# Two-layer hybrid decoder on one core: where in SBUF the split weights and the feed-forward products' operands lie

## The chip, the cores and the metric

The kernel runs on one core of one Trainium2 chip. The metric is the device time of one execution in microseconds.

## The reference

Two layers, x of 256 tokens by 1024 channels, float32. In each layer a token mixer and a feed-forward follow one another, each with a residual and a layer norm:

```python
proj = x @ w_in        # RNN input | RNN gate | q latent | kv latent | rotary key | gate A | gate B
y_rnn = gelu(g_rnn) * rg_lru(causal_dwconv(x_rnn), ...)
y_mla = mla_attention(q_lat, kv_lat, k_rope_raw, ...)      # 16 heads, causal
x = layer_norm(ALPHA * x + (sigmoid(gate_a) * y_rnn + sigmoid(gate_b) * y_mla) @ w_out)
h_gate, h_val = split(causal_dwconv(x @ w_up))             # 2 x 3072 channels
x = layer_norm(ALPHA * x + (gelu(h_gate) * h_val) @ w_down)
```

## The kernel before, in words

Every large product is made of three float32r matmuls. An operand is split into a high part (ScalarE, line 185 for weights, line 199 for activations) and the rest, the low part (VectorE, lines 186 and 200); `mm3` (lines 193 to 196) adds high by high, high by low and low by high.

Weights come in blocks of 2048 columns by a DMA on SP's queue into one of four `raw` buffers (line 156). `load_split` cuts a block into two halves of 1024 and gives each half a buffer that holds its high and its low part. Weights used as stationary operand go to the pool `wpool`, tag "w": six buffers, any half in any of them. The down-projection's and some other weights go to the general slots of 4,096 bytes (`slot`). A raw buffer is free for the next DMA when both halves are split, a weight buffer when TensorE has read it for the last time.

`proj_pair` computes 256 channels by 256 tokens: for each of two groups of 128 channels (m) it goes over the eight chunks kc of the 1024 input channels, with three matmuls each, so 48 matmuls of 128x256. Chunks 0 to 3 lie in the first half's buffer, 4 to 7 in the second's. The moving operand is x. There are 16 such pairs in a layer's mixer (branches g and x, gates A and B, four each) and 22 in its feed-forward; the feed-forward's first two of 24 pairs are done by tokens (`up_tok`, tile upt, weights moving).

In the feed-forward `up(j)` makes the pair, the convolution and the gated product, and splits that into `hh` and `hl` (tag "k1", 13 buffers of 1,024 bytes). From the sixth pair on, each pair is followed by `out_chunk`: 12 matmuls of 128x512 into `dacc`, with a piece of `hh` or `hl` as stationary operand and the down weights in slots as moving one. There are 48 chunks, 576 such matmuls; 36 pairs come right behind a product. The tag "k1" also holds the splits of the RNN branch's convolution (`xch`, `xcl`), the transposed layer norm (`lnx`) and the merged branches (`mg`).

TensorE's order is the program's: the mixer's steps are written out by hand in `ORDER` (x is a pair of the RNN branch, e its gates, h a pair of gate B, b, q, k, p a group of heads, v its values, s, f, y attention, o the output projection). Loads are issued on SP in program order. ScalarE's and VectorE's order is made by a planner when the program is built.

The addresses follow from the pools, which lie one behind the other. The six weight buffers begin at 58,560 bytes of each partition and are 8,320 bytes apart; 58,560 is 192 modulo 256 and 8,320 is 128 modulo 256, so they lie at 192 and 64 in turn. All slots, so x, the down weights and the mixers' results, and all "k1" buffers lie at 0 modulo 256. Which buffer a half gets is settled when the program is built. Of the 36 pairs behind a product, 12 have both halves at the same place modulo 256, 18 the first at 192 and the second at 64, and 6 the first at 64 and the second at 192. An offset inside a half is a multiple of 512 bytes in all pairs.

Of the kernel before, what the change touches and what calls it, by code (L numbers as in the profile page):

```python
# [11 lines left out]
F32 = mybir.dt.float32  # L12
F32R = mybir.dt.float32r
# [4 lines left out]
P = 128  # L18
D = 1024
S = 256  # L20
# [29 lines left out]
HELD = 4  # L50
WARM = 8
LINE = 256
STEP = 32
KORD = (0, 1, 4, 5, 2, 3, 6, 7)
NPAIR = DFF // P
ALPHA = (2 * DEPTH) ** 0.25
# [69 lines left out]
def trunk(ctx, tc, x_tok, x_chan, pos, wts, par, lnrow, consts, out):  # L126
# [8 lines left out]
    wpool = ctx.enter_context(tc.tile_pool(name="wpool", bufs=1))  # L135
    big = ctx.enter_context(tc.tile_pool(name="big", bufs=1))
    sm = ctx.enter_context(tc.tile_pool(name="sm", bufs=2))
    pp = ctx.enter_context(tc.tile_pool(name="pp", bufs=4, space=bass.MemoryType.PSUM))

    def slot(name, dt=F32):  # L140
# [20 lines left out]
    def behind(ins, first):  # L161
        if first is not None:
            tc.add_manual_dep(ins.ins, first.ins.name, no_sync, reason="issue order")

    last_split = [None]
    ready = [(None, None)]
    later = [False]

    def load_split(l, key, cuts, in_slots=False, after=(None, None),
                   step=1024, parts=None, between=None):  # L170
        raw = load_raw(l, key, parts, between)
        if later[0]:
            after = ready[0]
        n = WOFF[key][1]
        res = []
        for a, b in cuts:
            if in_slots:
                hi, lo = slot("wsh", F32R), slot("wsl", F32R)
            else:
                both = wpool.tile([P, 2048 + STEP], F32R, tag="w", name="w", bufs=6)  # L180
                hi, lo = both[:, :1024], both[:, 1024:2048]
            for c in range(a, b, step):
                d = min(c + step, b)
                h, w = hi[:, c - a:d - a], raw[:, c:d]
                behind(A.activation(h, w, AF.Copy), after[0])  # L185
                lo_ins = V.tensor_tensor(out=lo[:, c - a:d - a], in0=w, in1=h.bitcast(F32),  # L186
                                         op=ALU.subtract)
                behind(lo_ins, after[1])
                last_split[0] = lo_ins
            res.append((hi, lo))  # L190
        return res
# [186 lines left out]
    class LayerNorm:  # L378
# [48 lines left out]
        def turn(self, t):  # L427
            l, z = self.l, self.res[t]
            ts = slice(t * P, (t + 1) * P)
            pts = [bank("lnT") for _ in range(2)]  # L430
            for q in range(2):
                for c in range(4):
                    T.transpose(pts[q][:, c * P:(c + 1) * P],
                                z[:, (4 * q + c) * P:(4 * q + c + 1) * P], ident)
            ea = None
            for cc in range(2):
                for q in range(2):
                    hi, lo = (v.rearrange("p (c s) -> p c s", c=4) for v in self.xs[q])
                    xt = sm.tile([P, 2, P], F32, tag="k1", name="lnx", bufs=13, align_bytes=LINE)
                    hv, lv = hi[:, 2 * cc:2 * cc + 2, ts], lo[:, 2 * cc:2 * cc + 2, ts]  # L440
                    for e in range(2):
                        c = 2 * cc + e
                        gc = pcol(l, self.gn, 4 * q + c)
                        bc = pcol(l, self.bn, 4 * q + c)
                        src = pts[q][:, c * P:(c + 1) * P]
                        if q == 0:
                            V.tensor_scalar(out=xt[:, e], in0=src, scalar1=gc, scalar2=bc,
                                            op0=ALU.mult, op1=ALU.add)
                        else:
                            behind(A.activation(xt[:, e], src, AF.Identity, scale=gc, bias=bc),  # L450
                                   ea)
                    ea = A.activation(hv, xt, AF.Copy)
                    ev = V.tensor_tensor(out=lv, in0=xt, in1=hv.bitcast(F32), op=ALU.subtract)
            self.ends = (ea, ev)
# [56 lines left out]
    for l in range(DEPTH):  # L511
# [6 lines left out]
        def proj_pair(key, r=None):  # L518
            if r is None:
                if key not in held:  # L520
                    fetch(key)
                r = held.pop(key)
            ps = bank("proj")
            for m in range(2):
                for kc in range(KC):
                    hi, lo = r[kc // 4]
                    o = (kc % 4) * 256 + m * P
                    rh, rl = xsl(xs, kc)
                    mm3(ps[:, m * S:(m + 1) * S], hi[:, o:o + P], lo[:, o:o + P],
                        rh, rl, kc == 0, kc == KC - 1)  # L530
            return ps

        gl = [slot("gl") for _ in range(2)]
# [61 lines left out]
        def conv_branch(i):  # L595
            ps = proj_pair(("x", i))
            for m in range(2):
                c = 2 * i + m
                dst = xc[c // 4][:, (c % 4) * S:(c % 4) * S + S]
                src = ps[:, m * S:(m + 1) * S]  # L600
                A.activation(dst, src, AF.Identity, scale=pcol(l, "cw", 24 + c),
                             bias=pcol(l, "cb", c))
                for k in range(1, 4):
                    conv_end.append(V.scalar_tensor_tensor(
                        out=dst[:, k:], in0=src[:, :S - k], scalar=pcol(l, "cw", 8 * (3 - k) + c),
                        in1=dst[:, k:], op0=ALU.mult, op1=ALU.add,
                    ))
                xh = sm.tile([P, S], F32R, tag="k1", name="xch", bufs=13, align_bytes=LINE)
                xl = sm.tile([P, S], F32R, tag="k1", name="xcl", bufs=13, align_bytes=LINE)
                A.activation(xh, dst, AF.Copy)  # L610
                V.tensor_tensor(out=xl, in0=dst, in1=xh.bitcast(F32), op=ALU.subtract)
                xsp[c] = (xh, xl)
# [181 lines left out]
        def values(c):  # L794
            g, pr = divmod(c, 2)
            pts = pst.pop(c)
            vs = vts[g // 2][1]
            yps = bank("yps")
            for t in range(NT):
                for hh in range(2):  # L800
                    hv = t * 512 + (4 * (g % 2) + 2 * pr + hh) * 64
                    T.matmul(yps[hh * 64:hh * 64 + 64, t * P:S], lhsT=vs[:, hv:hv + 64],  # L802
                             rhs=pts[hh][:, 2 * t * P:(2 + t) * P],
                             start=t == 0, stop=t == 1)
            if mer[c // 4] is None:
                mer[c // 4] = (slot("mhi", F32R), slot("mlo", F32R))
            cs = slice((c % 4) * S, (c % 4) * S + S)
            mg = sm.tile([P, S], F32, tag="k1", name="mg", bufs=13, align_bytes=LINE)
            V.tensor_tensor(out=mg, in0=yps[:, :S], in1=sB[c // 4][:, cs], op=ALU.mult)
            V.tensor_tensor(out=mg, in0=mg, in1=r_t[c // 4][:, cs], op=ALU.add)  # L810
            split2(mer[c // 4][0][:, cs], mer[c // 4][1][:, cs], mg)
# [76 lines left out]
        def up(j):  # L888
            if j < NB:
                ps = turn(j)  # L890
            else:
                r = uw.pop(j, None)
                if r is None:
                    r = load_split(l, ("up", j), ((0, 1024), (1024, 2048)), after=convs[max(0, len(convs) - 4)])
                ps = proj_pair(("up", j), r)
            u = []
            for m in range(2):
                ch = m * NPAIR + j
                src = ps[:, m * S:(m + 1) * S]
                dst = sm.tile([P, S], F32, tag="k15", name=f"u{m}", bufs=7,  # L900
                              align_bytes=LINE)
                ea = A.activation(dst, src, AF.Identity, scale=pcol(l, "fw", 96 + ch),  # L902
                                  bias=pcol(l, "fb", ch))
                for k in range(1, 3):
                    ev = V.scalar_tensor_tensor(  # L905
                        out=dst[:, k:], in0=src[:, :S - k],
                        scalar=pcol(l, "fw", 48 * (2 - k) + ch),
                        in1=dst[:, k:], op0=ALU.mult, op1=ALU.add,
                    )
                u.append(dst)  # L910
            convs.append((ea, ev))
            A.activation(u[0], u[0], AF.Gelu_apprx_tanh)
            V.tensor_tensor(out=u[1], in0=u[1], in1=u[0], op=ALU.mult)  # L913
            mh = sm.tile([P, S], F32R, tag="k1", name="hh", bufs=13, align_bytes=LINE)
            ml = sm.tile([P, S], F32R, tag="k1", name="hl", bufs=13, align_bytes=LINE)
            split2(mh, ml, u[1])
            hq[j] = (mh, ml)

# [145 lines left out]
```

## Time and profile before

| | |
|---|---|
| three runs | 785.43, 785.65, 787.75 us; median 785.65 us |
| the profiled execution | 786.62 us, of which the span from the first to the last instruction is 784.76 us |
| TensorE, matmuls | busy 770.5 us of the span |
| VectorE, ScalarE | busy 646.0 us, 510.2 us |
| DMA | 144.76 MB, 184 GB/s on average |
| granted TensorE clock | 0.995 of full speed over the span |

How to read it: a matmul's time in the trace reaches from its start to the end of its results and overlaps with the next one; what a matmul costs in a row of matmuls is the distance from its start to the next one's start. The page's busy time counts overlapping matmuls once. Times in the timeline are in microseconds from the span's start.

### The profile page before, as it was taken

What the parts mean: (1) busy time and instruction counts of PE and PEld (TensorE: products, weight loads), DVE (VectorE), ACT (ScalarE), POOL (GpSimd) and SP (SyncE); (2) the same over time, 40 slices, a digit from 0 to 9 for tenths busy, and PEclk for the clock granted to TensorE, in tenths of its full rate; (3) what the DMA queues carried; (4) which work ended last, traced back from release to release, by engine and by line L of the source; (5) the groups of instructions that cost most, each with busy time, mean ns of one, the idle gap of its engine ahead of it and who ended that gap; (6) DMA issues with size and microseconds to landing.
All of it is one profiled execution on the core that took longest, in us unless ns stands there. A gap on an engine that the chain in (4) does not pass through costs nothing.

```text
span 784.8 us, 14452 instructions
## 1 busy us (share of the span) xinstructions
PE 770.5 (98%) x5712; PEld 723.9 (92%) x5712; DVE 646.0 (82%) x1260; ACT 510.2 (65%) x910; POOL 10.2 (1%) x27
## 2 busy tenths in 40 slices
PE   9999899999999999999999999999999999999996
PEld 9999899878999999999899999998799999999994
DVE  6998789997699977668777897999877998677665
ACT  6856887783677565556374579688657775565540
POOL 0000000000000000000000000000000000000000
PEclk9999999999999999999999999999999999999999
DMA  9855436525457555535715554463515675746311
GB/s 320 331 210 215 151 112 240 207 63 210 162 199 262 203 199 210 195 126 196 268 52 218 169 208 134 172 231 123 193 76 186 261 251 182 247 162 200 123 54 54
DMA packets 26467, 144.76 MB, mean 184 GB/s; under 512 B 3360, under 2 KB 7072, under 8 KB 11808
## 3 DMA queue, kind: packets, MB, share of 16 engines
q1 hardware_dynamic: 26400, 143.84, 51.7%
q8 instruction: 45, 0.74, 0.4%
q14 instruction: 22, 0.18, 0.1%
HBM read 140.68 MB, written 1.05 MB: 181 GB/s over the span
## 4 chain that ended last, share of the span: by engine, by line
PE 89%; DVE 4%; ACT 4%; issue 2%; DMA 1%; SPq 0%; DVEq 0%
PE proj L196 16%; PE proj L194 15%; PE proj L195 15%; PE dacc L194 6%; PE dacc L195 6%; PE dacc L196 6%; PE oacc L194 2%; PE oacc L196 2%; PE oacc L195 2%; PE sps L759 2%; DVE w L186 2%; PE yps L802 2%; PE ptp L787 1%; PE latp L195 1%; PE latp L196 1%
## 5 line engine op out<-in xcount | busy, mean ns | idle before, releaser
L196 PE MATMUL proj<-xhi,w 128*128 128x256 f32 x1216 | 338.0, 278 | 3.0 <-DVE w L186 3.0
L194 PE MATMUL proj<-xhi,w 128*128 128x256 f32 x1216 | 338.1, 278 | 0.0
L195 PE MATMUL proj<-xlo,w 128*128 128x256 f32 x1216 | 337.7, 278 | 0.0
L186 DVE TENSOR_TENSOR w<-raw,w 128x1024 fp32r<-128x1024 f32 (+5 forms) x226 | 241.8, 1087 | 52.4 <-ACT w L185 51.9
L185 ACT ACTIVATE w<-raw 128x1024 fp32r<-128x1024 f32 (+5 forms) x226 | 208.8, 952 | 86.6 <-PE proj L196 73.4
L196 PEld LDWEIGHTS proj<-xhi,w 128*128 128x128 f32 x1216 | 228.8, 188 | 3.4 <-DVE w L186 3.4
L195 PEld LDWEIGHTS proj<-xlo,w 128*128 128x128 f32 x1216 | 229.2, 189 | 1.3
L194 PEld LDWEIGHTS proj<-xhi,w 128*128 128x128 f32 x1216 | 228.9, 188 | 1.4
L905 DVE SCALAR_TENSOR_TENSOR u<-proj,par,u 128x255 f32<-128x255 f32 (+1 forms) x176 | 83.4, 478 | 25.4 <-ACT u L902 23.3
L902 ACT ACTIVATE u<-proj,par 128x256 f32<-128x256 f32 x88 | 49.7, 564 | 72.7 <-DVE u L905 47.8
L194 PE MATMUL dacc<-wsh,hh 128*128 128x512 f32 x192 | 75.2, 392 | 0.0
L195 PE MATMUL dacc<-wsl,hh 128*128 128x512 f32 x192 | 75.1, 391 | 0.0
L196 PE MATMUL dacc<-wsh,hl 128*128 128x512 f32 x192 | 74.7, 389 | 0.0
L186 DVE TENSOR_TENSOR wsl<-raw,wsh 128x1024 fp32r<-128x1024 f32 (+2 forms) x66 | 70.4, 1077 | 0.0
L185 ACT ACTIVATE wsh<-raw 128x1024 fp32r<-128x1024 f32 (+2 forms) x66 | 59.5, 938 | 0.0
L196 PEld LDWEIGHTS dacc<-wsh,hl 128*128 128x128 f32 x192 | 36.1, 188 | 7.8
L194 PEld LDWEIGHTS dacc<-wsh,hh 128*128 128x128 f32 x192 | 36.0, 188 | 6.4
L195 PEld LDWEIGHTS dacc<-wsl,hh 128*128 128x128 f32 x192 | 36.1, 188 | 6.0
L199 ACT ACTIVATE hh<-u 128x256 fp32r<-128x256 f32 x48 | 19.8, 411 | 24.7 <-DVE u L913 24.6
L194 PE MATMUL oacc<-w,mhi 128*128 128x512 f32 x64 | 26.7, 417 | 0.0
L196 PE MATMUL oacc<-w,mlo 128*128 128x512 f32 x64 | 25.3, 395 | 0.0
L195 PE MATMUL oacc<-w,mhi 128*128 128x512 f32 x64 | 25.2, 393 | 0.0
(213 smaller groups left out, 1130.2 us busy)
## 6 DMA issues: line engine op xcount, KB each, us to landing
raw<-in_wts SPq DMA_DIRECT2D x114, 1024.0 KB, 4.9
raw<-in_wts SPq DMA_DIRECT2D x8, 832.0 KB, 4.9
gb<-in_lnrow SPq DMA_DIRECT2D x8, 512.0 KB, 7.7
raw<-in_wts SPq DMA_DIRECT2D x4, 672.0 KB, 4.0
raw<-in_wts SPq DMA_DIRECT2D x7, 336.0 KB, 6.1
raw<-in_wts SPq DMA_DIRECT2D x4, 512.0 KB, 4.8
xres<-in_x_tok SPq DMA_DIRECT2D x2, 512.0 KB, 6.0
k<-krot SPq DMA_DIRECT2D x8, 128.0 KB, 2.4
```

Of the source, the lines that this page charges most:

```text
L185: behind(A.activation(h, w, AF.Copy), after[0])
L186: lo_ins = V.tensor_tensor(out=lo[:, c - a:d - a], in0=w, in1=h.bitcast(F32), op=ALU.subtract)
L194: T.matmul(o, lhsT=lh, rhs=rh, start=start, stop=False)
L195: T.matmul(o, lhsT=lh, rhs=rl, start=False, stop=False)
L196: T.matmul(o, lhsT=ll, rhs=rh, start=False, stop=stop)
L199: A.activation(hi, src, AF.Copy)
L759: T.matmul(sps[:, P:P + S], lhsT=q96[:, h4, P:], rhs=k96[:, h4], start=True, stop=True)
L787: T.transpose(ptp[:, b * P:(b + 1) * P], sns[hh][:, b * P:(b + 1) * P], ident)
L802: T.matmul(yps[hh * 64:hh * 64 + 64, t * P:S], lhsT=vs[:, hv:hv + 64], rhs=pts[hh][:, 2 * t * P:(2 + t) * P], start=t == 0, stop=t == 1)
L902: ea = A.activation(dst, src, AF.Identity, scale=pcol(l, "fw", 96 + ch), bias=pcol(l, "fb", ch))
L905: ev = V.scalar_tensor_tensor(out=dst[:, k:], in0=src[:, :S - k], scalar=pcol(l, "fw", 48 * (2 - k) + ch), in1=dst[:, k:], op0=ALU.mult, o ...
```

## The change

The weight pool has two tags of three buffers, w0 for the first half of a block and w1 for the second, of 8,192 bytes each, with a tile of 128 bytes between them that is never used. By the pools' arithmetic w0 lies at 192 and w1 at 64 modulo 256. `proj_pair` goes over the chunks in the order 0, 4, 5, 1, 2, 3, 6, 7. The tiles of tag "k1" move to a pool of their own behind the others, after an unused tile of 160 bytes, and lie at 128 modulo 256. Blocks with one cut (the values' weights) use w0 alone.

```diff
-STEP = 32
+GAP = 32
+PORD = (0, 4, 5, 1, 2, 3, 6, 7)
...
+    kpool = ctx.enter_context(tc.tile_pool(name="kpool", bufs=1))
+    kpool.tile([P, 40], F32, name="kgap")
...
-        for a, b in cuts:
+        for i, (a, b) in enumerate(cuts):
             if in_slots:
                 hi, lo = slot("wsh", F32R), slot("wsl", F32R)
             else:
-                both = wpool.tile([P, 2048 + STEP], F32R, tag="w", name="w", bufs=6)
+                if i and not gap:
+                    gap.append(wpool.tile([P, GAP], F32, name="gap"))
+                both = wpool.tile([P, 2048], F32R, tag=f"w{i % 2}", name=f"w{i % 2}", bufs=3)
                 hi, lo = both[:, :1024], both[:, 1024:2048]
...
-                    xt = sm.tile([P, 2, P], F32, tag="k1", name="lnx", bufs=13, align_bytes=LINE)
+                    xt = kpool.tile([P, 2, P], F32, tag="k1", name="lnx", bufs=13)
...
             for m in range(2):
-                for kc in range(KC):
+                for kc in PORD:
                     hi, lo = r[kc // 4]
                     o = (kc % 4) * 256 + m * P
                     rh, rl = xsl(xs, kc)
                     mm3(ps[:, m * S:(m + 1) * S], hi[:, o:o + P], lo[:, o:o + P],
-                        rh, rl, kc == 0, kc == KC - 1)
+                        rh, rl, kc == PORD[0], kc == PORD[-1])
...
-            mh = sm.tile([P, S], F32R, tag="k1", name="hh", bufs=13, align_bytes=LINE)
-            ml = sm.tile([P, S], F32R, tag="k1", name="hl", bufs=13, align_bytes=LINE)
+            mh = kpool.tile([P, S], F32R, tag="k1", name="hh", bufs=13)
+            ml = kpool.tile([P, S], F32R, tag="k1", name="hl", bufs=13)
```

The tiles `xch`, `xcl` and `mg` change in the same way as `lnx`.

## Rows read from the trace of the kernel before

**Rows 1.** The page's first part: busy us, share of the span, instructions of each engine.

```profile
PE 770.5 (98%) x5712; PEld 723.9 (92%) x5712; DVE 646.0 (82%) x1260; ACT 510.2 (65%) x910; POOL 10.2 (1%) x27
```

**Rows 2.** TensorE's waits: engine, line, for whom; us in total, times, longest.

```profile
PE proj L196 <- DVE w L186: 3.0, 2, 1.5
PE gates L195 <- DVE xcl L611: 1.9, 2, 1.4
```

**Rows 3.** Busy time by stage, both feed-forwards: us, each engine, clock, DMA share, GB/s.

```profile
227.00:377.00 150.00, 150.00 (x1081) 141.26 (x1080) 121.86 (x190) 91.45 (x138) 0.00 (x0) 1.00 0.59 209
...
612.00:760.00 148.00, 148.00 (x1076) 139.18 (x1075) 117.19 (x183) 86.69 (x131) 0.00 (x0) 1.00 0.55 192
```

**Rows 4.** TensorE's timeline (start, us): a pair's first matmul, the next pair's first.

```profile
216.08 0.28 PE L194 MATMUL proj<-xhi,w 128*128 128x256 f32 x1
...
221.52 0.28 PE L194 MATMUL proj<-xhi,w 128*128 128x256 f32 x1
```

**Rows 5.** TensorE's timeline: first matmul of a pair at 64 and 64, the product behind.

```profile
237.96 0.28 PE L194 MATMUL proj<-xhi,w 128*128 128x256 f32 x1
...
243.62 0.40 PE L194 MATMUL dacc<-wsh,hh 128*128 128x512 f32 x1
```

**Rows 6.** TensorE's timeline: pair at 192 and 64, its matmuls 1, 13, 16, the product behind.

```profile
229.71 0.28 PE L194 MATMUL proj<-xhi,w 128*128 128x256 f32 x1
...
231.12 0.28 PE L194 MATMUL proj<-xhi,w 128*128 128x256 f32 x1
...
231.48 0.28 PE L194 MATMUL proj<-xhi,w 128*128 128x256 f32 x1
...
235.22 0.40 PE L194 MATMUL dacc<-wsh,hh 128*128 128x512 f32 x1
```

**Rows 7.** TensorE's timeline: first matmul of a pair at 64 and 192, the product behind.

```profile
622.84 0.28 PE L194 MATMUL proj<-xhi,w 128*128 128x256 f32 x1
...
628.38 0.40 PE L194 MATMUL dacc<-wsh,hh 128*128 128x512 f32 x1
```

**Rows 8.** TensorE's timeline: first matmuls of layer 1's first and second pair.

```profile
410.08 0.28 PE L194 MATMUL proj<-xhi,w 128*128 128x256 f32 x1
...
415.73 0.28 PE L194 MATMUL proj<-xhi,w 128*128 128x256 f32 x1
```

**Rows 9.** TensorE's timeline: third gate-B pair of layers 0, 0 and 1, matmuls 3, 13, 3.

```profile
116.95 0.38 PE L196 MATMUL proj<-xhi,w 128*128 128x256 f32 x1 [1.51 <-DVE w L186]
...
118.24 0.28 PE L194 MATMUL proj<-xhi,w 128*128 128x256 f32 x1
...
502.05 0.38 PE L196 MATMUL proj<-xhi,w 128*128 128x256 f32 x1 [1.51 <-DVE w L186]
```

**Rows 10.** VectorE's timeline: splits around the third gate-B pair and layer 0's last pair.

```profile
113.56 5.34 DVE L186 TENSOR_TENSOR w<-raw,w 128x896 fp32r<-128x896 f32 x5
...
370.72 1.21 DVE L186 TENSOR_TENSOR w<-raw,w 128x1024 fp32r<-128x1024 f32 x1
```

**Rows 11.** ScalarE's timeline: a branch-x pair's first half, the second head group's queries.

```profile
64.87 1.06 ACT L185 ACTIVATE w<-raw 128x1024 fp32r<-128x1024 f32 x1 [2.61 <-issue]
...
114.73 0.84 ACT L185 ACTIVATE w<-raw 128x768 fp32r<-128x768 f32 x1
```

**Rows 12.** TensorE's timeline: matmuls 1 and 6 of the first feed-forward product.

```profile
226.96 0.40 PE L194 MATMUL dacc<-wsh,hh 128*128 128x512 f32 x1
...
228.12 0.39 PE L196 MATMUL dacc<-wsh,hl 128*128 128x512 f32 x1
```

**Rows 13.** TensorE's timeline: two matmuls of an output projection, four steps apart.

```profile
177.67 0.39 PE L195 MATMUL oacc<-w,mhi 128*128 128x512 f32 x1
...
178.60 0.39 PE L196 MATMUL oacc<-w,mlo 128*128 128x512 f32 x1
```

**Rows 14.** TensorE's timeline: two matmuls of the up-projection by tokens, four steps apart.

```profile
196.96 0.28 PE L194 MATMUL upt<-wsh,xhi 128*128 128x256 f32 x1
...
197.44 0.28 PE L195 MATMUL upt<-wsl,xhi 128*128 128x256 f32 x1
```

More of the change, by code (lines that the diff above doesn't have):

```diff
@@ L163, in behind @@
             tc.add_manual_dep(ins.ins, first.ins.name, no_sync, reason="issue order")
+    gap = []
     last_split = [None]
@@ L607, in conv_branch @@
                     ))
-                xh = sm.tile([P, S], F32R, tag="k1", name="xch", bufs=13, align_bytes=LINE)
-                xl = sm.tile([P, S], F32R, tag="k1", name="xcl", bufs=13, align_bytes=LINE)
+                xh = kpool.tile([P, S], F32R, tag="k1", name="xch", bufs=13)
+                xl = kpool.tile([P, S], F32R, tag="k1", name="xcl", bufs=13)
                 A.activation(xh, dst, AF.Copy)
@@ L807, in values @@
             cs = slice((c % 4) * S, (c % 4) * S + S)
-            mg = sm.tile([P, S], F32, tag="k1", name="mg", bufs=13, align_bytes=LINE)
+            mg = kpool.tile([P, S], F32, tag="k1", name="mg", bufs=13)
             V.tensor_tensor(out=mg, in0=yps[:, :S], in1=sB[c // 4][:, cs], op=ALU.mult)
```

## Prediction

> **What bounds the kernel now.** I read the page's first part, TensorE's waits and the busy time by stage, then the order of single matmuls in time. TensorE is busy 770.5 us, 98% of the span [rows 1]; what it waits for others inside the work is 3.0 us for weight splits and 1.9 us for the gates' input, all in the mixers [rows 2], the rest of its idle time lies at both ends of the program. In both feed-forward stretches it is busy without a break (150.00 of 150.00 us and 148.00 of 148.00), while VectorE has 28 and 31 us to spare [rows 3]. So the time is the sum of the steps from one matmul's start to the next, and the question is what sets a step.
>
> The same product, 128x256 of proj, has two steps. A whole pair (48 matmuls) took 221.52 - 216.08 = 5.44 us, 113.3 ns a step [rows 4]; another took 243.62 - 237.96 = 5.66 us, 117.9 ns [rows 5]. Shapes, operands, the granted clock (full, 2.4 GHz [rows 3]) and even the place of the weights are the same, both halves at 64 modulo 256, and neither pair holds a wait. What differs is what ran before: the quick pair follows a quick pair, the slow one a feed-forward product. So the step depends on a state that is carried from matmul to matmul, and the buffers show where it changes. A third pair, first half at 192 and second at 64, begins slow (12 matmuls in 231.12 - 229.71 = 1.41 us), takes 0.36 us for three more after the move to 64, and has 113.3 ns a step from there to its end (33 in 235.22 - 231.48 = 3.74 us): 5.51 us in all [rows 6]. With 64 first and 192 second it took 628.38 - 622.84 = 5.54 us [rows 7]: there the step falls only at the return to 64 in the middle. The starts of all 76 pairs follow this, but for one that is released only at its third quarter. Once quick, a pair stays quick through every change of buffer; a slow one is released by going from 192 to 64, not by going from 64 to 192, and one without a change stays slow to the end. Every pair that follows a feed-forward product begins slow.
>
> Of the 36 such pairs, 12 keep to one class (5.65 to 5.66 us, 0.21 over 5.44), 6 go from 64 to 192 (0.10 over), 18 from 192 to 64 (0.07 over), each kind within 0.01 us of its row [rows 4 to 7]: 2.5 + 0.6 + 1.3 = 4.4 us. In layer 1's mixer the first three pairs are slow throughout (the first from 410.08 to 415.73, 5.65 us [rows 8]), 0.6 us, and the pair after the long wait of layer 0 loses 0.2 us.
>
> **The change, part by part.**
>
> *Weight buffers and order.* By the sizes, w0 starts at 58,560 (192 modulo 256, three of 8,192 bytes keep that), the gap adds 128 bytes, so w1 is at 64. Every pair goes from 192 to 64. In the new order the first such move comes after 3 matmuls and not 12, and there are four in a pair. Taking rows 6 as the rule, a pair that begins slow loses 3 x 4.5 ns before the move and the three steps of 0.12 us after it (about 15 ns): 0.028 us. The 36 pairs go from 4.4 to 1.0 us: -3.4. The three of layer 1's mixer: -0.55; the one of layer 0: -0.15. Together **-4.1 us**.
>
> *The second half is wanted sooner.* Before, its first use comes 12 matmuls (1.36 us) into a pair, now 3 (0.34 us). Where weights are ready long ahead this costs nothing; the cover is the distance of several us from the split to its use in the proj stretches. It costs where a pair waits for its own split. In both mixers that is the third pair of branch gate B: its third matmul starts at 116.95 and 502.05, after VectorE has written the first half's low part [rows 9]. VectorE then has two of five splits in a row left (they end at 113.56 + 5.34 = 118.90 [rows 10]); the second half's low part is the fourth, done about 118.05 at some 1.15 us each, and as far behind in layer 1. Before, that half's first matmul started at 118.24 [rows 9]. Now its low part is wanted at 117.4, so TensorE, which issues in order, stands about 0.65 us longer in each layer: **+1.3 us**, 0 if VectorE's order puts that split sooner, +2.0 if the first split slips too. The last pair of layer 0's feed-forward has its second half's low part ready 0.4 us after the pair begins (at 370.72 + 1.21 = 371.93, and that pair then wants it 0.56 us after its begin at 371.51 [rows 10]); with its first half released later (next part) I add **+0.3**, between 0 and 0.7.
>
> *Three buffers for each half in place of six for all.* The first half's last read is now chunk 3 in sixth place, two chunks (0.68 us) later. ScalarE's split into that buffer waits for it: at 64.87 it had stood idle 2.61 us, until the pair then running had read its first half [rows 11]. There the chain runs on through VectorE to the gates, for which TensorE waits [rows 2]. So up to 0.65 us in layer 0; I take **+0.4**, from 0 (VectorE has rope work to put in) to 1.5 (two or three splits in a row late by 0.65 before that wait). In attention a value block and a held output block also take first-half buffers. The split of 114.73 [rows 11] then waits for the third gate-B pair's first half, some 7 us; behind it on ScalarE stand the queries' and keys' copies, unless the planner, which orders ScalarE and VectorE anew, puts them ahead. By the same count the weights are still ready 3 us or more before use, and SP's loads wait for raw buffers that the second half's split frees, as before. Nothing for those; +2 if the new order is worse.
>
> *Feed-forward products' stationary tiles from 0 to 128 modulo 256*, moving weights at 0. No row has a 512-wide matmul with the two 128 apart. Now a block of 12 takes 1.16 us for its first five steps, 232 ns each, and then settles at 227 (seven in 229.71 - 228.12 [rows 6, 12]). Over 38 blocks the first five lose up to 0.026 us each, some 0.9 us. Low end: that goes, -0.9. Upper end: the nearest row is the output projection, whose moving weights are 64 or 192 apart from the stationary operand and which doesn't settle: 0.93 us for four steps, 232 [rows 13], so +5 ns on the 7 to 12 steps of a block that are now at 227, some +2.2 us over 576 steps. Far end: a product with both at 0 takes 120 ns a step and not 113.3 (four in 0.48 us [rows 14]); in that proportion the 512-wide would take 240, +6.7. I take **0**, as settled runs there are the rule, and keep -0.9 and +6.7.
> The Trainium skill, "TensorE: Matmul & The Clock Gate", section "Back-to-back issue gap", gives N/2.4 + 2.5 ns, which is 215.8 for 512. By it 576 such steps have 6 us in hand; no 512-wide float32r step of this trace is under 225.
>
> *The other tiles in the new pool* (conv splits, normalised x, merged) are read by TensorE only in 96 gate matmuls: nothing, between -0.1 and +0.4.
>
> **Sum.** -4.1 + 1.3 + 0.3 + 0.4 + 0 = -2.1 us. The profiled execution took 786.62 (span 784.76 and 1.86 around it), so 784.5; the median of the three runs, 785.65, lies 0.97 below it, so **783.5 us**.
>
> **Rivals.**
> 1. *The products lose at 128.* Each of 576 steps on a path that TensorE alone sets becomes longer. For: the output projection doesn't settle with other offsets. Against: the products settle within five steps at 0. Price on the forecast: at 232 ns +2.2, 785.7; at 236, +4.5, 788.0; at 240, 790.2. It ends slower than before by over 0.3% from a mean of 236 ns. 0.17, half of it above 788.
> 2. *More is won.* The pairs start quick, as the stationary tile read just before now lies elsewhere (-1.0), the products lose their slow first steps (-0.9), and the two waits for the second half don't come (-1.3): 780.3. For: what a pair starts with follows what ran before it. Against: VectorE's order follows the program. 0.18.
> 3. *The addresses do nothing*, and the slow steps come from something else in those stretches. Against: the step falls at a move from 192 to 64 in 24 of the pairs behind a product and never at another place [rows 6, 7]. Then only the costs are left, +2.0: 787.7; with none of them 785.65. 0.05.
> The Trainium skill says this in "SBUF — State Buffer", section "Who interferes with whom": TensorE has separate read ports for weights and moving operand and never waits on anyone. By that rule the change would give nothing; rows 4 and 5 differ by 4% and speak against it.
> 4. *The mixers lose what the feed-forwards win*: late splits at the upper ends of their ranges, +2 to +3.5 beyond the sum: 785.5 to 787. 0.10.
>
> **How the numbers follow.** My sum holds with 0.50 (781.8 to 785.2). 0.3%, about what a measurement of this kernel can tell from no change, is 2.36 us: under 783.3 faster, over 788.0 slower. Faster: 0.25 of the forecast's 0.50, 0.18 of rival 2: 0.43. Slower: 0.09 of rival 1 and some 0.03 of 3 and 4: 0.12. The same: 0.45. The range takes in rival 2 to 780.0 and rival 1 to 236 ns, 788.0.
>
> **What would show it.** Right: every pair after a product in 5.45 to 5.48 us, with 113 to 114 from about its seventh matmul; layer 1's first three pairs near 5.44; third gate-B pairs with a second wait of some 0.6 us; products at 226.7. Wrong: pairs still at 5.51 or above (the move from 192 to 64 is not what releases them), product blocks over 2.76 us, or TensorE idle in the feed-forward stretches (splits late).

## The result, and the profile after

The change made the kernel slower: 793.35 us (median of four runs, 792.51 to 794.05) against 786.29 on the same chip, ratio 1.0086 with a 95% interval of 1.0072 to 1.0101. The forecast was 783.5 us, the range 780.0 to 788.0. The profiled execution of the changed kernel has a span of 791.2 us, the one of before 784.8, and those 6.4 us are what has to be found. "The third gate-B pair" is, here as in the prediction, the one numbered 3 from 0: the last of the four to run, after the first head group has begun. Line numbers of the changed kernel are those of before plus 6.

The page's first part, then TensorE's waits (engine, line, for whom; us in total, times, longest), of the changed kernel:

```profile
PE 772.5 (98%) x5712; PEld 722.8 (91%) x5712; DVE 647.1 (82%) x1260; ACT 504.9 (64%) x910; POOL 10.9 (1%) x27
```

```profile
PE proj L202 <- DVE w L192: 5.6, 3, 2.7
PE gates L201 <- DVE xcl L617: 3.5, 2, 2.2
...
PE latp L200 <- ACT w L191: 0.7, 1, 0.7
```

TensorE is busy 98% of the span as before and is still the bound [rows 1]. Its waits for splits went from 3.0 to 5.6 us and those of the gates from 1.9 to 3.5 [rows 2]. Cut at the starts of the pairs, the difference lies here (us; the pairs of a layer are numbered in the order in which they run, the third gate-B pair is 15):

```
stretch                                      before   after
start to layer 0's first pair                  21.0    21.4   +0.4
layer 0  pairs 0 to 7                          46.3    46.8   +0.5
         pairs 8 to 10 with gates              24.9    23.6   -1.3
         pairs 11 to 14                        22.8    23.0   +0.2
         third gate-B pair and attention       89.1    91.9   +2.8
         feed-forward, first four pairs        25.6    25.5   -0.1
         feed-forward, the rest, to layer 1   180.4   179.4   -1.0
layer 1  pairs 0 to 7                          46.9    46.3   -0.6
         pairs 8 to 10 with gates              20.4    22.6   +2.2
         pairs 11 to 14                        22.8    23.0   +0.2
         third gate-B pair and attention       89.0    91.9   +2.9
         feed-forward, first four pairs        25.5    25.5    0.0
         feed-forward, to its last pair       140.5   140.4   -0.1
end                                            29.6    30.0   +0.3
```

**The feed-forwards** do what was forecast of the pairs, and lose it again in the products. The timeline of TensorE in the changed kernel (start, us): first matmul of the first product, of the pair behind it and of the next product.

```profile
229.43 0.39 PE L200 MATMUL dacc<-wsh,hh 128*128 128x512 f32 x1
...
232.22 0.28 PE L200 MATMUL proj<-xhi,w 128*128 128x256 f32 x1
...
237.69 0.39 PE L200 MATMUL dacc<-wsh,hh 128*128 128x512 f32 x1
```

The pair takes 237.69 - 232.22 = 5.47 us, and 35 of the 36 pairs behind a product take that (5.51, 5.55 or 5.65 before [rows 5 to 7]); all 36 together 197.2 us in place of 200.2 (197.15 and 200.25). The product's 12 steps take 232.22 - 229.43 = 2.79 us, 232.5 ns each, and so it stays: 575 steps took 133.7 us, 131.3 before. By stage (us, then busy time of TensorE, its weight loads, VectorE, ScalarE, GpSimd, granted clock, DMA share, GB/s), two feed-forward stretches and one of four us behind the start of layer 0's third gate-B pair:

```profile
118.00:122.00 4.00, 4.00 (x21) 4.00 (x22) 3.97 (x8) 0.00 (x0) 0.00 (x0) 0.58 0.95 365
...
233.00:377.00 144.00, 144.00 (x1052) 134.97 (x1052) 115.99 (x181) 86.75 (x135) 0.00 (x0) 1.00 0.59 208
621.00:769.00 148.00, 148.00 (x1079) 138.65 (x1078) 116.88 (x181) 85.37 (x132) 0.00 (x0) 1.00 0.53 187
```

The feed-forwards are without a break, as before [rows 3]. The first line is where the mixers lose.

**The third gate-B pair** of layer 0 on TensorE, then VectorE, then ScalarE, in the changed kernel (idle time ahead and what ended it in brackets):

```profile
114.88 0.28 PE L200 MATMUL proj<-xhi,w 128*128 128x256 f32 x1
...
117.94 0.39 PE L202 MATMUL proj<-xhi,w 128*128 128x256 f32 x1 [2.68 <-DVE w L192]
```

```profile
113.42 5.48 DVE L192 TENSOR_TENSOR w<-raw,w 128x896 fp32r<-128x896 f32 x5
```

```profile
111.48 1.07 ACT L191 ACTIVATE w<-raw 128x1024 fp32r<-128x1024 f32 x1
113.38 1.06 ACT L191 ACTIVATE w<-raw 128x1024 fp32r<-128x1024 f32 x1 [0.82 <-PE proj L202]
```

Both 1,024-wide splits are this pair's. The one at 111.48 is its *second* half; the first half comes at 113.38, after 0.82 us of waiting for TensorE. In VectorE's five splits in a row, which begin as before [rows 10], the first half's low part is fourth instead of third, and the third matmul starts 117.94 - 114.88 = 3.06 us into the pair (before, idle 1.51 [rows 9]). The 0.82 us on ScalarE is not itself what TensorE waits for: ScalarE is done with the first half at 113.38 + 1.06 = 114.44, and VectorE's third split begins only at 115.54. TensorE waits because the planner put this half's low part fourth. ScalarE before, in the same place, had taken the first half first and waited for TensorE only ahead of the second:

```profile
111.64 1.06 ACT L185 ACTIVATE w<-raw 128x1024 fp32r<-128x1024 f32 x1
112.87 1.06 ACT L185 ACTIVATE w<-raw 128x1024 fp32r<-128x1024 f32 x1 [0.17 <-PE proj L196]
```

Behind the wait 16 matmuls have a step of 213 ns: the granted clock is 0.58 over these four us, so it was at the lower level, 1.2 GHz, for most of them. Before, it was full there:

```profile
117.00:121.00 4.00, 4.00 (x34) 4.00 (x35) 3.97 (x8) 0.00 (x0) 0.00 (x0) 1.00 0.95 386
```

The pair takes 10.09 us in place of 7.43, in layer 1 10.03 in place of 7.22.

**The gates of layer 1.** ScalarE before, at 468 us, then in the changed kernel at the same place, then TensorE in the changed kernel:

```profile
468.05 1.06 ACT L185 ACTIVATE w<-raw 128x1024 fp32r<-128x1024 f32 x1 [2.09 <-PE proj L196]
469.01 0.40 ACT L610 ACTIVATE xch<-xc 128x256 fp32r<-128x256 f32 x1
469.41 1.07 ACT L185 ACTIVATE w<-raw 128x1024 fp32r<-128x1024 f32 x1
```

```profile
469.80 2.01 ACT L191 ACTIVATE w<-raw 128x1024 fp32r<-128x1024 f32 x2 [2.21 <-PE proj L202]
471.71 0.58 ACT L635 ACTIVATE sg<-proj 128x512 f32<-128x512 f32 x1
472.18 0.41 ACT L616 ACTIVATE xch<-xc 128x256 fp32r<-128x256 f32 x1
```

```profile
472.64 0.38 PE L200 MATMUL gates<-xch,w 128*128 128x256 f32 x1
474.24 0.39 PE L201 MATMUL gates<-xcl,w 128*128 128x256 f32 x1 [1.22 <-DVE xcl L617]
```

In the new order both halves of a pair are read to nearly its end, so their buffers come free close together; the planner puts both next splits in a row, and the gates' input, which stood between them, behind them. TensorE waits for it. This wait is new; layer 0's wait for the gates, 2.2 us in one piece, is about what its two pieces of 0.5 and 1.4 were before.

### The profile page after: what moved, and what is told of

Its sections match the earlier page's. It is cut to its first block, busy times and chain, and to the rows that moved or that the text cites. A ratio compares the mean times of both kernels' runs of the same rounds, so it can differ in the third digit from the quotient of the medians.

```text
span 791.2 us, 14456 instructions
## 1 busy us (share of the span) xinstructions
PE 772.5 (98%) x5712; PEld 722.8 (91%) x5712; DVE 647.1 (82%) x1260; ACT 504.9 (64%) x910; POOL 10.9 (1%) x27
## 4 chain that ended last, share of the span: by engine, by line
PE 86%; DVE 5%; ACT 4%; issue 2%; DMA 1%; SPq 0%; POOL 0%; DVEq 0%; ACTq 0%
PE proj L202 15%; PE proj L201 15%; PE proj L200 15%; PE dacc L200 6%; PE dacc L201 6%; PE dacc L202 6%; DVE w L192 2%; PE oacc L200 2%; PE oacc L202 2%; PE oacc L201 2%; PE sps L765 2%; PE yps L808 2%; PE ptp L793 1%; ACT w L191 1%; PE sps L763 1%
```

## The experiments

The theory after this look: the three parts are separate. The products lose 2.4 us by their place alone; three buffers for each half lengthen the wait of the third gate-B pair; the order makes the gates of layer 1 wait; and TensorE's lower clock behind a long wait makes each of these dearer. The rivals: the order alone does the harm, or the waits only move time that a later wait has to spare. The places modulo 256 are computed from the pools, the traces show no addresses. The kernel of before took 787.33 us beside the first four runs (median), 786.34 beside the next four and 786.95 beside the last three.

**Products back at 0 modulo 256.**

```diff
-    kpool.tile([P, 40], F32, name="kgap")
+    kpool.tile([P, 8], F32, name="kgap")
```

> The changed kernel with the k1 tiles back at 0 modulo 256, and nothing else undone. Theory A (the stationary tiles at 128 cost the products their settled 227 ns a step): products go from 232.5 ns a step to about 228, 576 x 4.3 ns = -2.5 us, and the pairs behind a gate step (5.52 us) go back to 5.44, six of them, -0.5 us; so about 790.3. Theory B (the loss lies wholly in the mixers): no change, 793.3. The feed-forward pairs stay near 5.47 us in both.

790.13 us, ratio to before 1.0048 (1.0031 to 1.0065). The first product's first matmul and the next pair's:

```profile
231.61 0.40 PE L200 MATMUL dacc<-wsh,hh 128*128 128x512 f32 x1
...
234.35 0.28 PE L200 MATMUL proj<-xhi,w 128*128 128x256 f32 x1
```

2.74 us, 228.3 ns a step, as before the change; all 575 steps 131.45 us. Pairs behind a product keep 5.47. Five of the six pairs behind a gates step, whose input lies in the same pool, go from 5.52 back to 5.44 us (the sixth, layer 0's pair 10, runs at half clock in this profile). That is 2.3 and 0.4 us of the 3.2 gained; the long waits remain. That is what theory A had.

**The old order of the chunks.**

```diff
-PORD = (0, 4, 5, 1, 2, 3, 6, 7)
+PORD = (0, 1, 2, 3, 4, 5, 6, 7)
```

> The changed kernel with the chunks in the order 0 to 7 again; buffers and tiles as changed. Theory A (the new order keeps the first half's buffer 0.68 us longer, so its split comes behind the second half's, the third gate-B pair waits 2.95 us and not 1.8, and TensorE's clock falls after it): the wait goes back to about 1.8 us, no half clock behind it, -2.7 us in each layer; gates' wait of layer 1 (2.0 us) goes; feed-forward pairs go from 5.471 to 5.507, +1.3 us; about 787. Theory B (three and three buffers make the splits late, whatever the order): the long waits stay, and with the slower pairs it is 794.5.

791.78 us, 1.0064 (1.0041 to 1.0087). The third matmul of the third gate-B pair, and TensorE's wait for the gates:

```profile
119.14 0.39 PE L202 MATMUL proj<-xhi,w 128*128 128x256 f32 x1 [2.65 <-DVE w L192]
```

```profile
PE gates L201 <- DVE xcl L617: 1.4, 1, 1.4
```

The long wait stays, so it isn't the order's; but behind it there are no slow matmuls in this profile, and the pair takes 8.42 us in both layers. (This profile is of an execution of 790.49 us at a mean clock of 0.994; the slowest took 795.08 at 0.989, so others may have had them.) The gates' wait of layer 1 is gone (one wait, that of layer 0): the stretch takes 20.95 us, not 22.6. That wait is the order's. So the long wait is as theory B has it, the gates as theory A; neither had the time.

**The order alone**, on the kernel of before: its six buffers, its places, only `PORD` in place of the loop over the chunks.

> The kernel before with the chunk order alone; six shared buffers, k1 tiles at 0. Theory A (order): the third gate-B pair waits near 3 us in both layers with the half clock behind it, and the mixers lose some 5 us as in the changed kernel; the feed-forward gains less than in the changed kernel where both halves lie in one class: about 789 to 791. Theory B (the split of the buffers is what makes the splits late): the mixers lose the second half's earlier need alone, +1.3 us, and the time is near 786.

797.49 us, 1.0127 (1.0104 to 1.015), slower than the whole change. TensorE's waits:

```profile
PE proj L197 <- DVE w L187: 4.7, 6, 1.5
PE gates L196 <- DVE xcl L612: 3.8, 3, 2.2
PE yps L803 <- ACT pT L791: 1.3, 2, 0.7
...
PE oacc L195 <- DVE k L733: 1.0, 2, 0.5
```

No wait over 1.5 us for a split, but six of them: the third gate-B pair of layer 0 stops for its first half and again for its second and takes 8.03 us, 0.61 more than before. Layer 1's ran at half clock behind the second stop (9.56 us). The gates' wait of layer 1 is here too, and attention takes 91.5 and 93.3 us with its pair, and has waits of its own. Theory A had waits near 3 us, theory B a time near 786: both fall. Pairs with both halves in one class still take 5.65 us, so the order without the buffers wins little.

**High and low parts 128 bytes apart**, in the kernel of before, where the buffer is 128 bytes longer than it needs; nothing else is changed.

```diff
-                hi, lo = both[:, :1024], both[:, 1024:2048]
+                hi, lo = both[:, :1024], both[:, 1024 + STEP:]
```

> The kernel before, with the low part of each weight buffer 128 bytes further, so that high and low part lie at 192 and 64 (or 64 and 192) in every half; nothing else. Theory A (a slow stretch is released by a step from 192 to 64): every pair has such a step within its first three matmuls, all 36 pairs behind a product go to about 5.46 to 5.48, none stays at 5.65, -3.3 us, mixers of layer 1 -0.5: about 782.5. Theory B (the place as such matters, and a change at every third matmul upsets the quick stretches): pairs between 5.44 and 5.66 throughout, 786 or more.

**782.55 us (781.99 to 782.96), 0.994 (0.9924 to 0.9957)**: faster than both kernels. A pair with both halves at 64, of the kind that took 5.66 us [rows 5], and the waits:

```profile
238.48 0.28 PE L194 MATMUL proj<-xhi,w 128*128 128x256 f32 x1
...
243.94 0.40 PE L194 MATMUL dacc<-wsh,hh 128*128 128x512 f32 x1
```

```profile
PE proj L196 <- DVE w L186: 3.0, 2, 1.5
PE gates L195 <- DVE xcl L611: 2.0, 2, 1.4
```

5.46 us; the others 5.45, and all 36 together 196.3 us in place of 200.2. What the change sought by moving buffers and chunks is had inside the buffer, with no load, split or matmul moved, and the mixers' waits stay those of before.

**The buffers alone**: the changed kernel with the old order and the products at 0 (both edits shown above).

> The changed kernel with the chunks in the old order and the products' tiles back at 0 modulo 256: three buffers for each half alone. Theory A (the long wait of the last gate-B pair comes from the three and three buffers, the products' place costs 2.4 us by itself): the wait stays at 2.9 us in both layers, products 228 to 229 ns a step, pairs behind a product 5.51 us, no wait for the gates' input beyond that of before; time 791.8 - 2.4 = 789.4 us, less up to 1.0 where pairs behind a gates step are quick again: 788.4 to 789.4. Theory B (the buffers only cost together with the other two parts): no wait longer than before's, 785.5 to 787.

788.67 us, 1.0033 (1.0021 to 1.0044): theory A. The third gate-B pair's third matmul, then the clock over 3 us behind it in layers 0 and 1:

```profile
118.22 0.39 PE L202 MATMUL proj<-xhi,w 128*128 128x256 f32 x1 [2.65 <-DVE w L192]
```

```profile
118.20:121.20 3.00, 2.98 (x25) 2.98 (x26) 2.97 (x7) 0.00 (x0) 0.00 (x0) 1.00 0.96 385
502.20:505.20 3.00, 2.95 (x14) 2.95 (x15) 2.97 (x7) 0.00 (x0) 0.00 (x0) 0.50 0.93 343
```

The step is 2.93 us in both layers; the clock falls to half behind it in layer 1 (14 matmuls in 3 us) and not in layer 0 (25). The pairs take 8.51 us in layer 0 and 9.94 in layer 1. The feed-forwards win 1.6 and 0.2 us (178.8 and 140.3), the two pairs lose 3.8.

**Value blocks in the second half's buffers.** Why is the first half late? In program order the attention's first value block is loaded shortly ahead of the third gate-B pair. Before, that pair's first half had a buffer that was free at 108.8 us and its second half the one of the pair just ahead, free at 112.8 (last reads on TensorE, the buffers by the pools' turns). With three buffers for first halves the value block takes the one that is free early, at 107.9, and leaves the first half that of the pair just ahead, free at 113.3.

```diff
+            h = 1 if key[0] == "v" else i % 2
...
-                both = wpool.tile([P, 2048], F32R, tag=f"w{i % 2}", name=f"w{i % 2}", bufs=3)
+                both = wpool.tile([P, 2048], F32R, tag=f"w{h}", name=f"w{h}", bufs=3)
```

> The changed kernel with the attention's value blocks in the second half's three buffers. Theory A (the value block takes the buffer that the last gate-B pair's first half had before, and leaves it that of the pair just ahead, which is free only 1.6 us before that pair starts): the first half's split comes 1.5 us or more sooner, the wait at the third matmul is 1.8 us or less, a second wait of about 0.6 us for the second half follows, no half clock, the pair takes 8.0 instead of 10.1 us, attention 89.8 instead of 91.9 in each layer: 793.35 - 4.1 = 789.3 us. Theory B (the planner's order on VectorE and ScalarE sets the wait, whatever the buffers): wait 2.9 us as in the changed kernel, 793.3 us.

798.21 us, 1.015 (1.0134 to 1.0166). Matmuls 3 and 6 of the third gate-B pair:

```profile
115.24 0.39 PE L203 MATMUL proj<-xhi,w 128*128 128x256 f32 x1 [0.35 <-DVE w L193]
...
118.38 0.58 PE L203 MATMUL proj<-xhi,w 128*128 128x256 f32 x1 [2.52 <-DVE w L193]
```

VectorE's five splits in a row around it:

```profile
112.99 5.34 DVE L193 TENSOR_TENSOR w<-raw,w 128x896 fp32r<-128x896 f32 x5
```

The first half's wait is gone, as theory A had it (0.35 us left). But now the *second* half has to take the buffer of the pair just ahead; VectorE writes its low part last of the five, to 112.99 + 5.34 = 118.33, behind the second head group's queries. Its wait is 2.52 us where 0.6 was expected, with half clock behind it (10.4 and 10.6 us a pair); attention waits too and takes 94.2 and 94.5 us with the pair. So where the value block goes decides which half is late. How late it is follows from VectorE's order, which the planner made anew with the buffers; no run keeps the buffers and changes that order, so the two are not told apart.

**TensorE kept busy in the wait.** Six matmuls of zeros ahead of the third gate-B pair, in its own PSUM bank:

```diff
             ps = bank("proj")
+            if key == ("gb", 3):
+                for _ in range(6):
+                    T.matmul(ps[:, :P], lhsT=idle, rhs=idle, start=True, stop=True)
```

> The changed kernel with six matmuls of zeros (2.56 us by the rows at the start of the program) ahead of the last gate-B pair of each layer, in its own bank, so that TensorE works through the wait of 2.96 us. Theory A (TensorE's idle time there lowers its clock, and the 16 or 17 matmuls at 213 ns cost 1.6 us in each layer): no half clock behind the wait, the pair takes 8.4 us less what the filling takes, attention 90.3 instead of 91.9, 793.35 - 3.2 = 790.1 us. Theory B (what the slow matmuls cost is taken back by later waits in attention): the half clock goes and the time stays at 793.3 us. Theory C (the clock falls for another reason): 16 slow matmuls remain, 793.3 us or more.

791.06 us (788.78 to 791.09), 1.005 (1.0032 to 1.0067), where the changed kernel had 793.35. The six matmuls (12 in the profile), then the pair's first and third, and the clock behind them:

```profile
116.30 1.50 PE L532 MATMUL proj<-idle 128*128 128x128 f32 x12
117.55 0.36 PE L200 MATMUL proj<-xhi,w 128*128 128x256 f32 x1
...
119.35 0.38 PE L202 MATMUL proj<-xhi,w 128*128 128x256 f32 x1 [1.31 <-DVE w L192]
```

```profile
119.40:123.40 4.00, 4.00 (x35) 4.00 (x36) 3.97 (x8) 0.00 (x0) 0.00 (x0) 1.00 0.90 340
```

The third matmul still comes 119.35 - 116.30 = 3.05 us after TensorE gets there, but the clock stays at 1.00 (0.58 without the six) and the pair takes 8.37 and 8.36 us with the filling. Attention with its pair goes from 91.9 to 90.2 and 90.3: the fall of the clock cost 1.6 to 1.7 us in each layer, as by theory A. The six took 1.25 us, half of what I had from the start of the program. Of the 3.3 us the median shows 2.3; in this profile layer 0's pair 10 lost 1.1 behind its own wait at half clock.

**Where the products' tiles may lie.** On the kernel with high and low apart (782.55 us), the products' pool at 192, then at 64 modulo 256 (`kgap` of 24 and 56 floats).

> The kernel of before with high and low parts 128 bytes apart in each weight buffer (782.55 us), and the products' stationary tiles at 192 modulo 256 in place of 0. Theory A (any place but the moving weights' own costs the products 4 ns a step): dacc 232 to 233 ns, 782.55 + 2.4 = 785.0 us. Theory B (only the place 128 away costs): 226.7 to 228.6 ns, 781.5 to 782.6 us.

> As with the products' stationary tiles at 192 modulo 256 (782.9 us), but at 64. There the 25 pairs behind a product whose first weights lie at 192 took 5440 ns, and the 11 that begin at 64 took 5492. Theory A (a pair begins quick where its first weights lie at the place modulo 256 where the product's stationary tiles lay): now the 11 take 5440 and the 25 take 5492, 14 x 0.052 = 0.7 us more, 783.6 us. Theory B (it is the place 192 of the pair itself that is quick): as before, 25 quick and 11 slow, 782.9 us. Products 229 ns a step by both.

At 192: 782.9 us, 0.9953 (0.9938 to 0.9967), products 229.1 ns a step. At 64: 784.8 us, 0.9973 (0.9961 to 0.9986), products 232.9. With 0 (228.6) and 128 (232.5) above, both theories of the first run fall, A by 192 and B by 64: 0 and 192 are near each other, 64 and 128 cost 4 ns. A pair behind a product at 192, first with its weights at 192, then at 64, and the products behind:

```profile
229.85 0.28 PE L196 MATMUL proj<-xhi,w 128*128 128x256 f32 x1
...
235.29 0.39 PE L196 MATMUL dacc<-wsh,hh 128*128 128x512 f32 x1
...
238.04 0.28 PE L196 MATMUL proj<-xhi,w 128*128 128x256 f32 x1
...
243.53 0.39 PE L196 MATMUL dacc<-wsh,hh 128*128 128x512 f32 x1
```

5.44 and 5.49 us. With the products at 64 the pairs at 64 take 5.445 and those at 192 5.452: the first is theory A's, the second is not (5.492 expected), and neither theory had the products' 232.9.

**All six buffers at 192**, with the products at 192 as above, and on top of it five matmuls of zeros in the last gates step of layer 0.

```diff
-                both = wpool.tile([P, 2048 + STEP], F32R, tag="w", name="w", bufs=6)
-                hi, lo = both[:, :1024], both[:, 1024 + STEP:]
+                both = wpool.tile([P, 2048 + 2 * STEP], F32R, tag="w", name="w", bufs=6)
+                hi, lo = both[:, :1024], both[:, 1024 + STEP:2048 + STEP]
```

> High and low parts 128 bytes apart, products' tiles at 192, and all six weight buffers at 192 (64 for the low part), order of chunks as before. Theory A (the state is settled by the places of the matmuls themselves, high at 192 and low at 64 in turn): all 36 pairs behind a product 5440 ns, 11 x 0.052 = 0.6 us less than with mixed buffers, 782.3 us. Theory B (a change of place from one buffer to the next is what releases a slow pair): pairs that begin slow, those behind gates and transposes above all, stay slow to their end, 5651 ns, and the time rises to 783.5 us or more.

> The kernel with all buffers at 192, and in layer 0 five matmuls of zeros (one and four, 2.1 us) where the last gates step waits 0.8 and 2.3 us for its input. Theory A (TensorE's idle time there lowers its clock and the matmuls at 213 ns behind it cost 1.0 to 1.6 us): the pair behind that step goes from some 6.4 to 7.1 us to 5.44 to 5.5, 781.0 us. Theory B (the clock falls whatever TensorE does there, or a later wait takes the gain): 782.3 us.

782.97 us, 0.9955 (0.9941 to 0.997), and 782.67 us, 0.995 (0.9936 to 0.9963): no gain over 782.55. All 36 pairs behind a product take 5.44 us, as by theory A; but in the mixers most pairs that begin slow stay slow to the end, and pairs 10 to 14 of both layers hand it on, as by theory B (layer 1's first pair was quick after three matmuls). Starts of pairs 11 and 12 of layer 0 in the first of the two, then the waits for splits in the first and in the second:

```profile
91.19 0.28 PE L196 MATMUL proj<-xhi,w 128*128 128x256 f32 x1
...
96.90 0.28 PE L196 MATMUL proj<-xhi,w 128*128 128x256 f32 x1
```

```profile
PE proj L198 <- DVE w L188: 0.8, 2, 0.4
```

```profile
PE proj L198 <- DVE w L188: 2.4, 3, 1.5
```

5.71 us a pair. The zeros make layer 0's five pairs quick (5.44), and the time doesn't fall: the third gate-B pair, whose third matmul came 0.67 us after its second in the first, has 1.80 there in the second. From pair 10's start to the feed-forward it is 117.9 and 117.7 us. So in these two profiles layer 0's mixer up to that pair is set by the splits of ScalarE and VectorE; TensorE's time there is worth nothing until they are sooner. What these two runs can't tell is the price of the lower clock behind the gates, since pair 10 had full clock without the zeros as well.

## Why the prediction was wrong

1. *Weight buffers and order*, -4.1: right where it was largest. 35 of the 36 pairs behind a product take 5.471 us, 5.468 was forecast; the 36 fell by 3.1 us with the layer's last pair in them, which takes 5.67 as it waits for its second half (0.2, +0.3 in the sum). Layer 1's first eight pairs gained 0.6 (0.55 forecast). The rule behind the figure is too wide: the six pairs behind a gates step also move from 192 to 64 after 3 matmuls, and are released only at the next such move, after 18 (5.52 us); with all buffers at 192 pairs 10 to 14 make that move in every chunk, from the high to the low part, and stay slow to their end.
2. *Products at 128*, taken as 0: mis-sized. The step is 232.5 ns and the block costs 2.79 us; +2.4, at the bound of +2.2 that the output projection gave [rows 13]. That was rival 1 at its first price. I chose "as settled runs there are the rule"; the blocks at 128 never settle. With the pairs it leaves -0.7 of -3.1 in the feed-forwards.
3. *The second half is wanted sooner*, +1.3: the mechanism is real (0.61 us in the run with the order alone, 0.65 forecast), but in the changed kernel it isn't what happens. There the first half slips by 1.17 us in each layer (idle 2.68 for 1.51), where the upper end of +2.0 had allowed 0.35, and hides the second's wait.
4. *Three buffers for each half*, +0.4, in the mixers nothing more: this is the step that failed. I followed the value block's first-half buffer one load too late: I had the second head group's queries wait for the third gate-B pair's buffer, and overlooked that the value block had already left that pair the buffer of the one ahead. The row of the split that waits 0.82 us for TensorE agrees with it, and the run with the value blocks elsewhere moves the wait to the other half. And the planner's freedom, which the sum counted as help ("unless the planner puts them ahead"), put the second half's split first, and in layer 1 both splits ahead of the gates' input: +2.2, which by the runs with and without the new order is the order's and not the three buffers'. For the waits of both mixers the sum had +0.4 here and +1.3 in (3); measured, the third gate-B pairs with attention cost 2.8 and 2.9, of which 1.6 each is the clock's (5), and the gates of layer 1 cost 2.2. That the planner's order follows from the buffers is likely and not shown by itself.
5. *No term for the clock.* The sum priced waits at their length. A pair behind a wait of 2.9 us paid 1.6 on top, in both layers of this profile. It need not: behind the same wait the profile with the old order has full clock in both layers, the one with the buffers alone in one. What decides it stays open. Behind the 1.8 us of before the clock was 1.00, but the same trace had a fall behind the gates' wait of layer 0, where pair 10 took 6.44 us, and I didn't carry it over to a longer wait.

So +2.8 and +2.9 in the third gate-B pairs with attention, +2.2 in the gates of layer 1, +2.4 in products, against -3.1 in pairs and -1.3 around layer 0's gates. The last is this profile's luck: pair 10 has full clock in it, 5.52 us for 6.44, and in two other profiles with the same buffers and order (products at 0; TensorE kept busy) that stretch took 25.2 us. Rival 4, the mixers lose what the feed-forwards win, came with rival 1; it stopped at +3.5. Rival 3 fell: the low part's 128 bytes alone gain 4.8 us. The Trainium skill's "SBUF — State Buffer", section "Who interferes with whom", states that TensorE never waits on anyone; it speaks of engines that use memory at the same time and not of where an operand lies. Read as saying that the place can't matter, it doesn't agree with these runs: a step of the same product takes 228.6 or 232.9 ns by the place of its stationary tile. Whether TensorE's own two reads get in each other's way there, or another engine's, no run here shows.

The parts don't add up: the order alone cost 10.2 us, the buffers alone 2.3, the products about 3, and together 7.1. The likely reason is that each moves splits for which another part then has to wait; no run shows that by itself.

## What to carry to other kernels

Change an address by moving data inside its buffer before changing rings, counts or order: the same quick state came for 128 bytes and no moved wait. When a ring of buffers is divided, list for each load which earlier tile frees its buffer, value blocks and other odd loads included, and look for one that gets the tile just ahead. Where TensorE waits, give a forecast also the price of the matmuls behind the wait at the lower clock, and where a later wait has time to spare, price the gain ahead of it at nothing.

## What I had not expected of the hardware

- The step of a 512-wide float32r product depends on its stationary tile's place modulo 256, moving weights at 0: 228.6 ns at 0, 232.9 at 64, 232.5 at 128, 229.1 at 192 (means of 575 steps). All tiles of the pool are 1,024 bytes apart, so that 256 is the period is not shown for them.
- A wait of the same length (the next matmul starts 2.93 us after the last) is followed by half clock in one layer and full clock in the other, in one execution (the buffers alone); behind a wait filled with matmuls of zeros it stayed full in both.
- The slow state outlives whole pairs. With all buffers at 192 and the low part at 64, pairs 10 to 14 of a mixer took 5.71 us each though two steps of three move between the two places, which with mixed buffers and the products at 0 released the pairs behind a product within six matmuls. What sets and ends that state is open: going from 192 to 64, as the prediction had it, isn't enough.
